# Two layers of a hybrid decoder: the other model of the builder puts the instructions in order

## The chip, the cores and the metric

The kernel runs on one core of a Trainium2 chip. TensorE (PE in the profile) does the matmuls and transposes, VectorE (DVE), ScalarE (ACT) and GpSimd (POOL) the element-wise work, and the queue of SyncE (SP) issues the loads. The metric is device time in microseconds (us), the median of several executions. The builder writes one row of instructions for each engine; in the trace an instruction that waits stands before all that follow it in its row.

## The reference

One step of a decoder with two layers over 560 columns: 32 decoded tokens (8 sequences of 4), 16 meta tokens and a prompt of 512. The channel width is 1024. One layer is:

```
x = x + 0.5 * swiglu(rmsnorm(x), ffn1_w_in, ffn1_w_out)      # inner width 2816
h = rmsnorm(x);  columns = h @ w_mix_in                       # one projection for three groups of heads
fox_o = forgetting attention, 4 heads of 64, bias = sums of log forget gates, paged cache of 512 per sequence
ssd_o = state-space scan, 8 heads of 64 in chunks of 128, causal convolution of width 4, gate, grouped rmsnorm
gla_o = gated linear attention, 4 heads (32, 64), gate per channel, rmsnorm per head, gate
x = x + concat(fox_o, ssd_o, gla_o) @ w_mix_out
x = x + 0.5 * swiglu(rmsnorm(x), ffn2_w_in, ffn2_w_out)
```

The outputs are x for prompt and decoded tokens and, per layer, the new keys, values, log forget gates and the states of the convolution, the scan and the linear attention.

## The kernel before

**Tiling.** x lies transposed in on-chip memory, [128, 8, 560] in fp32: eight blocks of 128 channels. Its columns are two groups, A (304: decode, meta and the first 256 of the prompt) and B (256: the rest). A matrix product is made of three matmuls per block (`mm3`): each operand is split into a high part, rounded to the matmul's input type, and a low part, the rest; high by high, high by low and low by high are summed. `hhiA`, `hloA`, `hhiB`, `hloB` are the parts of the normed activations, `whi` and `wlo` those of a block of weights, `keep` those of blocks that both groups use at a stage's edge. `unit` makes them: a load from SP, a copy on ACT (high), a subtraction on DVE or POOL (low).

**Stages.** Per layer: ffn 1, the mix, ffn 2; then the next layer. An ffn is almost all matmuls. `norm` (and `first_norm` at the start) squares and sums x, multiplies by a column of ones to sum over channels (`ps<-c_ones,s`, one column wide), forms the root on POOL (`nr`), spreads it by a transpose (`ps<-c_ident,nr`), and writes the split activations.

**The mix.** Its steps are generators, run in the order of a hand-written list, a step to each name:

```
MIX_ORDER = """
fox_in:A fox_in:A ssd_in:A fox_in:A gla_in:A gla_in:A O:A gla_in:A fox_norm:A fox_norm:B gla:4 decode:A fox:0
fox:4 gla:0 gla:1 fox:1 ssd_in:A ssd_in:A ssd_in:A ssd:4 ssd:0 ssd:1 gla_in:B gla_in:B gla_in:B ssd_in:B
ssd_in:B ssd_in:B ssd_in:B split:A O:B gla:2 fox:3 ssd:2 gla:3 out:A out:A fox:2 ssd:3 out:A split:B out:A
out:B out:B norm:A out:B out:B norm:B
"""
```

`fox_in`, `ssd_in` and `gla_in` are the input projections (A, B: the group), `fox:`, `ssd:` and `gla:` with a number are the mixers of one tile of columns (0 to 3 the prompt in blocks of 128, 4 decode and meta), `split` splits the mixers' outputs, and `out` is the output projection. The scan (`ssd`) and the linear attention (`gla`) of a tile need the state of the tile before. A mixer's step is a chain: a few matmuls or transposes, DVE or ACT on the result, matmuls again.

**What sets the order.** The program is written for one thread. The builder (`tile.TileContext`) takes the instructions in the order of the program as their order of preference, runs a model of the engines, and puts on each engine's row the first of its instructions that the model says is ready. So the row of an engine is fixed when the program is built, and a wrong guess in the model is not mended on the chip. `BUFS` and the pools of PSUM (two banks of psg for projections, three each of psL and psF for mixers) limit how far ahead it may go.

Nearly all instructions are recorded under the lines of small helpers: L265 matmul (`mm`), L269 transpose (`tr`), L272 and L275 DVE or POOL (`tt`, `stt`), L278 ACT (`act`), L310 POOL's root (`rpow`).

Of the kernel before, what the change touches and what calls it, by code (L numbers as in the profile page):

```python
# [1414 lines left out]
def build():  # L1415
    nc = _bacc.Bacc("TRN2", target_bir_lowering=False, num_devices=1, dynamic_dma_scratch_size=1024)
    a = {n: nc.dram_tensor(n, s, F32, kind="ExternalInput").ap() for n, s in INS.items()}
    a["pt"] = nc.dram_tensor("pt", (1, 32), I32, kind="ExternalInput").ap()
    for n, s in OUTS.items():
        a[n] = nc.dram_tensor(n, s, F32, kind="ExternalOutput").ap()  # L1420
    with tile.TileContext(nc) as tc, ExitStack() as es:
        Trunk(tc, a, es).run()
    nc.finalize()
    return nc
# [61 lines left out]
```

## Time and profile before

| | us |
|---|---|
| median of 3 runs | 2452.31 (2452.1 to 2452.59) |
| profiled execution | 2455.32 |
| its span in the profile | 2453.5 |

The profiled execution is one of its own, 3.0 us above the median of the runs. The page's first section gives busy time per engine; a stretch is read by comparing its length with PE's busy time in it, and by the granted clock beside it, which is 1.00 at 2.4 GHz and 0.5 at 1.2 GHz. By time: ffn 1 of layer 0 until about 450 us, the mix of layer 0 with its projections until 840 us, ffn 2 and the next ffn 1 until 1650 us, the mix of layer 1 until 2060 us, the last ffn until the end.

### The profile page before, as it was taken

The numbers are of one execution on the slowest core, as the hardware profiler recorded it, in microseconds if no ns is written. First come the engines' busy times: TensorE is split into PE (matmuls) and PEld (weight loads), VectorE is DVE, ScalarE is ACT, GpSimd is POOL, SyncE is SP. The second block draws the span as 40 slices with busy tenths as digits, with TensorE's granted clock in tenths as the row PEclk, the third lists the DMA queues.
The fourth block names the chain that finished last, engine by engine and source line by source line (L and its number), as shares of the span: only waits on it lengthen the run. The fifth ranks groups of instructions, "written<-read, shape, count | busy, mean of one in ns | idle before, by whom it ended". The sixth has DMA issues, their size and how long they took to land. (4 is left out here: it accounts for less than half of the span.)

```text
span 2453.5 us, 44862 instructions
## 1 busy us (share of the span) xinstructions
PE 2368.8 (97%) x17908; PEld 2254.9 (92%) x17908; DVE 1256.3 (51%) x2675; ACT 869.7 (35%) x1902; POOL 523.7 (21%) x688
## 2 busy tenths in 40 slices
PE   8999999999889999999999999999998999999999
PEld 8999999987777899999999999999776779999999
DVE  5434345388788533333443333343888985333333
ACT  4323223444354432322333232334343544323231
POOL 3202124233232310100221010131423324101010
PEclk9999999989899999999999999999899999999999
DMA  4222223344322322222222222232443222222222
GB/s 150 88 87 87 87 86 96 95 123 135 116 79 66 106 85 86 87 87 86 87 78 86 86 85 83 87 101 86 129 135 102 88 90 87 87 86 87 87 84 84
DMA packets 89683, 230.57 MB, mean 94 GB/s; under 512 B 12706, under 2 KB 38050, under 8 KB 89474
## 3 DMA queue, kind: packets, MB, share of 16 engines
q1 hardware_dynamic: 89042, 227.54, 29.9%
q8 instruction: 141, 2.31, 0.4%
q14 instruction: 68, 0.56, 0.1%
q10 hardware_dynamic: 432, 0.16, 0.0%
HBM read 219.73 MB, written 7.92 MB: 93 GB/s over the span
## 5 line engine op out<-in xcount | busy, mean ns | idle before, releaser
L272 DVE TENSOR_TENSOR wlo<-raw,whi 128x512 fp32r<-128x512 f32 (+1 forms) x649 | 464.1, 718 | 404.5 <-ACT whi L278 395.1
L278 ACT ACTIVATE whi<-raw 128x512 fp32r<-128x512 f32 (+1 forms) x680 | 427.0, 631 | 646.0 <-PE ps L265 589.3
L265 PE MATMUL ps<-hhiA,wlo 128*128 128x304 f32 x1664 | 507.5, 305 | 0.0
L265 PE MATMUL ps<-hhiA,whi 128*128 128x304 f32 x1664 | 506.8, 305 | 0.0
L265 PE MATMUL ps<-hloA,whi 128*128 128x304 f32 x1664 | 505.6, 304 | 0.0
L265 PE MATMUL ps<-hhiB,wlo 128*128 128x256 f32 x1664 | 471.2, 283 | 4.4 <-POOL wlo L272 3.0
L265 PE MATMUL ps<-hhiB,whi 128*128 128x256 f32 x1664 | 469.6, 283 | 2.0 <-ACT s L278 0.9
L265 PE MATMUL ps<-hloB,whi 128*128 128x256 f32 x1664 | 469.5, 282 | 0.0
L265 PEld LDWEIGHTS ps<-hhiB,whi 128*128 128x128 f32 x1664 | 315.0, 189 | 6.1 <-issue 1.9
L265 PEld LDWEIGHTS ps<-hhiB,wlo 128*128 128x128 f32 x1664 | 315.2, 190 | 5.6 <-POOL wlo L272 3.2
L265 PEld LDWEIGHTS ps<-hhiA,wlo 128*128 128x128 f32 x1664 | 314.8, 189 | 3.9 <-issue 3.0
L265 PEld LDWEIGHTS ps<-hloA,whi 128*128 128x128 f32 x1664 | 315.3, 189 | 2.8 <-issue 2.0
L265 PEld LDWEIGHTS ps<-hhiA,whi 128*128 128x128 f32 x1664 | 314.7, 189 | 2.6 <-issue 1.4
L265 PEld LDWEIGHTS ps<-hloB,whi 128*128 128x128 f32 x1664 | 314.5, 189 | 2.3 <-issue 1.5
L272 POOL TENSOR_TENSOR hidA<-s,hidA 128x304 fp32r<-128x304 f32 x88 | 76.0, 864 | 849.2 <-ACT hidA L278 849.1
L265 PE MATMUL ps<-hidA,whi 128*128 128x304 f32 x1072 | 226.2, 302 | 0.0
L275 DVE SCALAR_TENSOR_TENSOR x<-ps,x 128x304 f32<-128x304 f32 (+1 forms) x192 | 86.0, 449 | 232.3 <-PE ps L265 230.7
L265 PE MATMUL ps<-hidB,whi 128*128 128x256 f32 x1072 | 193.9, 281 | 0.0
L265 PEld LDWEIGHTS ps<-hidA,whi 128*128 128x128 f32 x1072 | 174.4, 188 | 0.0
L265 PEld LDWEIGHTS ps<-hidB,whi 128*128 128x128 f32 x1072 | 166.2, 189 | 0.0
L272 DVE TENSOR_TENSOR s<-s,ps 128x256 f32<-128x256 f32 (+3 forms) x194 | 90.4, 467 | 145.7 <-PE ps L265 137.6
L265 PE MATMUL ps<-hidA,wlo 128*128 128x304 f32 x536 | 162.1, 302 | 0.0
(334 smaller groups left out, 3579.9 us busy)
## 6 DMA issues: line engine op xcount, KB each, us to landing
raw<-win SPq DMA_DIRECT2D x176, 512.0 KB, 3.5
raw<-wout SPq DMA_DIRECT2D x64, 512.0 KB, 3.5
raw<-wfm SPq DMA_DIRECT2D x48, 512.0 KB, 3.5
raw<-wmo SPq DMA_DIRECT2D x32, 512.0 KB, 3.6
raw<-wout SPq DMA_DIRECT2D x32, 384.0 KB, 3.5
pg<-kpage SPq DMA_DIRECT2D x64, 130.0 KB, 2.2
pg<-vpage SPq DMA_DIRECT2D x64, 128.0 KB, 2.3
raw<-wtm SPq DMA_DIRECT2D x8, 544.0 KB
```

The costliest lines, as they stand in the source:

```text
L265: return self.T.matmul(out, lhsT, rhs, start=start, stop=stop, **k)
L272: return (eng or self.V).tensor_tensor(out=out, in0=a, in1=b, op=op)
L275: return self.V.scalar_tensor_tensor(out=out, in0=a, scalar=s, in1=b, op0=op0, op1=op1)
L278: return self.S.activation(out, in_, f, **k)
```

## The change

The builder's other model of the machine is used to make the rows. The instructions, their operands and their data are the same.

```diff
@@ -1418,7 +1418,7 @@
-    with tile.TileContext(nc) as tc, ExitStack() as es:
+    with tile.TileContext(nc, schedule_with_timeline_sim=True) as tc, ExitStack() as es:
         Trunk(tc, a, es).run()
```

On PE, the rows of the ffn stages keep their order but for the ends of a stage. Three places follow, on PE; in a row stands the line, the operation, output<-inputs with the program's numbers, and the size.

The first is at the start, where group B's matmuls with the kept weights run. `ps_354<-c_ones` are the sums of B's norm, `ps_362<-c_ident,nr` its transposes; `ps_366`, `ps_391`, `ps_427` and `ps_452` are projections of the first ffn. Before:

```order
L265 MATMUL ps_366<-hhiB_314,whi_274 128x256
L265 MATMUL ps_366<-hloB_315,whi_274 128x256
L265 MATMUL ps_354<-c_ones_82,s_57_332 128x1
L265 MATMUL ps_354<-c_ones_82,s_58_334 128x1
L265 MATMUL ps_354<-c_ones_82,s_57_332 128x1
L265 MATMUL ps_354<-c_ones_82,s_58_334 128x1
L265 MATMUL ps_366<-hhiB_314,wlo_275 128x256
L265 MATMUL ps_366<-hhiB_314,whi_274 128x256
L265 MATMUL ps_366<-hloB_315,whi_274 128x256
L265 MATMUL ps_366<-hhiB_314,wlo_275 128x256
L269 MATMUL ps_362<-c_ident_80,nr_359 128x128 x2
L265 MATMUL ps_391<-hhiB_314,keep_235 128x256
```

Now:

```order
L265 MATMUL ps_427<-hhiB_314,keep_110 128x256
L265 MATMUL ps_427<-hloB_315,keep_110 128x256
L265 MATMUL ps_354<-c_ones_82,s_57_332 128x1
L265 MATMUL ps_354<-c_ones_82,s_58_334 128x1
L265 MATMUL ps_354<-c_ones_82,s_57_332 128x1
L265 MATMUL ps_354<-c_ones_82,s_58_334 128x1
L265 MATMUL ps_427<-hhiB_314,keep_111 128x256
L265 MATMUL ps_427<-hhiB_314,keep_110 128x256
...
L265 MATMUL ps_452<-hloB_315,keep_97 128x256
L265 MATMUL ps_452<-hhiB_314,keep_98 128x256
L269 MATMUL ps_362<-c_ident_80,nr_359 128x128 x2
L265 MATMUL ps_452<-hhiB_314,keep_97 128x256
```

B's sums now stand some 40 matmuls later, behind `ps_391` and most of `ps_427`, and its transposes come 28 matmuls behind the sums instead of 4.

The second is in the middle of layer 0's mix. `ps_7694`, `ps_7700` and `ps_7704` belong to ssd:0 (`c_strict_r` is a constant mask, `s_1309` and its like come from DVE or POOL), `ps_8039` and `ps_8077` to projections of group B, `ps_8709` to `ps_8722` to fox:3. Before:

```order
L269 MATMUL ps_7694<-c_ident_80,xc_1186_7155 128x128
L265 MATMUL ps_8039<-hloB_4888,whi_8035 128x256
L265 MATMUL ps_8039<-hhiB_4887,wlo_8036 128x256
L265 MATMUL ps_8077<-hhiB_4887,wlo_8070 128x256
L265 MATMUL ps_8077<-hhiB_4887,whi_8069 128x256
L265 MATMUL ps_8077<-hloB_4888,whi_8069 128x256
L265 MATMUL ps_7700<-scz_7698,xc_1186_7155 128x256
...
L265 MATMUL ps_8077<-hloB_4888,whi_8073 128x256
L265 MATMUL ps_8077<-hhiB_4887,wlo_8074 128x256
L265 MATMUL ps_7704<-s_1309_7705,c_strict_r_490 128x512
L265 MATMUL ps_7704<-s_1310_7708,c_strict_r_490 128x512
L265 MATMUL ps_8077<-hhiB_4887,whi_8073 128x256
```

Now:

```order
L269 MATMUL ps_7694<-c_ident_80,xc_1186_7155 128x128
L265 MATMUL ps_7700<-scz_7698,xc_1186_7155 128x256
L265 MATMUL ps_7704<-s_1309_7705,c_strict_r_490 128x512
L269 MATMUL ps_8709<-c_ident_80,f_1538_8701 128x128 x3
L269 MATMUL ps_8716<-c_ident_80,f_1538_8701 128x128
L265 MATMUL ps_8720<-kaug_984,qaug_985 128x400
L265 MATMUL ps_7704<-s_1310_7708,c_strict_r_490 128x512
L269 MATMUL ps_8709<-c_ident_80,f_1539_8703 128x128
L265 MATMUL ps_8722<-kaug_984,qaug_985 128x128
...
L265 MATMUL ps_8722<-c_cmask_r_494,c_identb_978 128x128
L265 MATMUL ps_7714<-s_1313_7715,c_strict_r_490 128x512
L265 MATMUL ps_7714<-s_1314_7718,c_strict_r_490 128x512
```

The projections between the steps of ssd:0 are gone from here (they stand earlier), and steps of fox:3 stand in their place.

The third is the end of layer 0's mix. `ps_9294`, `ps_9304`, `ps_9314`, `ps_9324`, `ps_9332` and `ps_9348` belong to ssd:3, `ps_9454` is an output projection of group A, `ps_9526` and `ps_9562` are two of group B. Before:

```order
L265 MATMUL ps_9294<-s_1708_9295,c_strict_r_490 128x512
L265 MATMUL ps_9294<-s_1709_9298,c_strict_r_490 128x512
L265 MATMUL ps_9454<-hloA_8568,whi_9446 128x304
L265 MATMUL ps_9454<-hhiA_8567,wlo_9447 128x304
L265 MATMUL ps_9454<-hhiA_8567,whi_9446 128x304
L265 MATMUL ps_9454<-hloA_8568,whi_9446 128x304
...
L265 MATMUL ps_9454<-hhiA_8567,wlo_9451 128x304
L265 MATMUL ps_9454<-hhiA_8567,whi_9450 128x304
L265 MATMUL ps_9304<-s_1712_9305,c_strict_r_490 128x512
L265 MATMUL ps_9304<-s_1713_9308,c_strict_r_490 128x512
L265 MATMUL ps_9314<-s_1700_9280,s_1710_9301 128x64 x4
L265 MATMUL ps_9324<-Ssd_71,scz_9288 128x256
```

Now:

```order
L265 MATMUL ps_9290<-scz_9288,xc_1432_8251 128x256
L265 MATMUL ps_9294<-s_1708_9295,c_strict_r_490 128x512
L265 MATMUL ps_9294<-s_1709_9298,c_strict_r_490 128x512
L265 MATMUL ps_9304<-s_1712_9305,c_strict_r_490 128x512
L265 MATMUL ps_9304<-s_1713_9308,c_strict_r_490 128x512
L265 MATMUL ps_9314<-s_1700_9280,s_1710_9301 128x64 x4
L265 MATMUL ps_9324<-Ssd_71,scz_9288 128x256 x2
L265 MATMUL ps_9314<-s_1700_9280,s_1714_9311 128x64 x4
L265 MATMUL ps_9332<-s_1718_9330,sbt_9286 64x256 x2
L269 MATMUL ps_9348<-c_ident_80,s_1701_9282 128x128 x4
L265 MATMUL ps_9526<-hhiB_9426,whi_9518 128x256
L265 MATMUL ps_9562<-hhiB_9426,whi_9554 128x256
```

The output projections of A have moved ahead of this, ssd:3 stands in one piece, and those of B follow it.

## Rows read from the trace of the kernel before

**Rows 1.** The page's span and totals: busy time, share of the span, instructions.

```profile
span 2453.5 us, 44862 instructions
...
PE 2368.8 (97%) x17908; PEld 2254.9 (92%) x17908; DVE 1256.3 (51%) x2675; ACT 869.7 (35%) x1902; POOL 523.7 (21%) x688
```

**Rows 2.** Stretches: length, PE, PEld, DVE, ACT, POOL busy (count), clock, DMA share, GB/s.

```profile
...
420.00:450.00 30.00, 28.70 (x241) 27.97 (x239) 14.54 (x43) 12.81 (x35) 17.87 (x33) 1.00 0.26 72
516.50:608.00 91.50, 86.75 (x668) 66.43 (x667) 75.15 (x216) 34.67 (x95) 34.83 (x78) 0.91 0.45 133
608.00:668.00 60.00, 54.22 (x369) 43.97 (x367) 46.24 (x107) 23.25 (x62) 16.08 (x15) 0.94 0.37 115
668.00:746.60 78.60, 69.98 (x474) 59.80 (x475) 68.62 (x164) 41.08 (x110) 27.75 (x33) 0.93 0.24 78
746.60:791.20 44.60, 40.24 (x254) 31.55 (x252) 36.40 (x77) 20.11 (x56) 12.90 (x13) 1.00 0.21 68
791.20:818.30 27.10, 25.06 (x202) 23.97 (x200) 20.53 (x38) 15.09 (x33) 11.47 (x12) 1.00 0.38 125
818.30:840.00 21.70, 18.22 (x121) 17.48 (x121) 14.81 (x28) 10.47 (x24) 11.07 (x13) 0.92 0.42 136
840.00:1200.00 360.00, 360.00 (x2799) 360.00 (x2798) 133.90 (x236) 106.98 (x204) 36.48 (x43) 1.00 0.29 90
...
1734.00:1827.00 93.00, 85.89 (x672) 65.81 (x671) 75.41 (x224) 36.03 (x99) 33.91 (x78) 0.93 0.45 132
1827.00:1887.00 60.00, 53.78 (x374) 42.41 (x373) 47.78 (x107) 24.42 (x68) 17.15 (x14) 1.00 0.36 116
1887.00:1963.60 76.60, 67.39 (x466) 57.26 (x466) 69.26 (x161) 39.35 (x105) 28.86 (x33) 0.98 0.25 77
1963.60:2008.00 44.40, 40.62 (x255) 31.75 (x253) 37.27 (x77) 20.09 (x55) 12.75 (x13) 1.00 0.20 66
2008.00:2035.00 27.00, 25.30 (x203) 24.06 (x201) 20.54 (x37) 14.79 (x32) 11.65 (x12) 1.00 0.40 131
2035.00:2060.00 25.00, 21.15 (x144) 20.69 (x145) 16.04 (x30) 11.17 (x24) 10.91 (x12) 0.93 0.36 113
```

**Rows 3.** Waits of PE, its timeline and one stretch at the start.

```profile
PE ps L265 <- ACT keep L278: 6.4, 1, 6.4
...
32.41 1.05 PE L265 MATMUL ps<-c_ones,s 128*128 128x1 f32 x8 [1.62 <-DVE s L272]
...
34.90 0.69 PE L269 MATMUL ps<-c_ident,nr 128*128 128x128 f32 x2 [0.85 <-POOL nr L310]
...
35.00:42.00 7.00, 7.00 (x38) 7.00 (x39) 1.78 (x5) 0.90 (x3) 0.00 (x0) 0.58 0.44 150
```

**Rows 4.** Waits of PE in the whole span and at 1200 to 1250 us; that stretch.

```profile
PE ps L265 <- DMA pg<-vpage: 0.4, 1, 0.4
...
PE ps L265 <- DVE s L272: 2.1, 1, 2.1
...
1200.00:1250.00 50.00, 46.86 (x355) 45.95 (x355) 26.50 (x52) 19.37 (x44) 23.20 (x27) 1.00 0.16 53
```

**Rows 5.** The stretch of the middle steps; DVE's timeline at its first and last instruction.

```profile
607.60:717.50 109.90, 96.59 (x641) 80.54 (x641) 90.01 (x213) 51.28 (x135) 34.39 (x40) 0.92 0.32 99
...
656.94 0.41 DVE L275 SCALAR_TENSOR_TENSOR gg<-gg,ps 128x256 f32<-128x256 f32 x1
...
670.53 1.15 DVE L272 TENSOR_TENSOR s<-c_tri,dr 128x512 fp32r<-128x512 f32 x1
```

**Rows 6.** PE's groups in 746.6 to 791.2 us; DVE's timeline there (start, us).

```profile
L265 PE MATMUL ps<-hloA,whi 128*128 128x304 f32 x36 | 11.8, 327 | 0.0
...
744.67 1.02 DVE L1136 TENSOR_SCALAR s<-s,sss 128x256 f32<-128x256 f32 x2
...
790.29 0.62 DVE L1136 TENSOR_SCALAR s<-s,sss 128x256 f32<-128x256 f32 x2 [0.82 <-POOL sss L310]
```

## The prediction

> **What bounds the kernel now.** I read the totals of the page first, then busy time by stretch, then TensorE's (PE's) waits, then single rows. PE is busy 2368.8 us of a span of 2453.5 us [rows 1], so all that an order can change is the idle 84.7 us and the clock at which the rest runs. By stretch, the feed-forward stages are full: 360.00 of 360 us at full clock between 840 and 1200 us, with VectorE (DVE) at 133.90 us [rows 2]. There no order can win, and only a bad one can lose. The idle time lies in both layers' mixing stages. Layer 0's six stretches from 516.5 to 840 us lose 4.75 + 5.78 + 8.62 + 4.36 + 2.04 + 3.48 = 29.03 us (length less PE's busy time), layer 1's six from 1734 to 2060 us 7.11 + 6.22 + 9.21 + 3.78 + 1.70 + 3.85 = 31.87 us [rows 2]. In the same stretches DVE is busy about 80% of the time, and the matmuls that keep PE going are mostly not the mixers' own: they are input and output projections, placed between the mixers' dependent steps. I call them cover. Which of them stand where is what the change decides.
>
> **The change part by part.** Instructions and data are the same; only places in each engine's row differ. The feed-forward stages stand as before, but for their first and last rows. That leaves four kinds of places.
>
> *Start.* PE stops for 1.6 us at group B's first norm (waiting for DVE's s) and for 0.85 us at nr, and then has a stretch of 7 us at a granted clock of 0.58 [rows 3]. The new order puts group B's sum matmuls and transposes some 40 and 65 matmuls later, by which time their inputs are there. If the two stops at B go, and the 7 us behind them come to the full clock (7 × 0.42 = 2.9 us), the start gains up to 1.6 + 0.85 + 2.9 = 5.4 us. Against it, ScalarE and DVE split some kept weights later, behind B's norm; PE already waits once for such a split, 6.4 us [rows 3]; and SyncE's queue issues the second block of input weights behind small constants. Another wait half as long would cost 3.2 us and leave the start at +3 with nothing gained. (Elsewhere loads have slack: all of PE's waits for a DMA in the span are one of 0.4 us [rows 4].) I take −2, between the ends and nearer to the stops that visibly go.
>
> *Norms at the hand-overs.* At 1200 to 1250 us PE loses 3.14 us, of which 2.1 us are one wait for the norm's s [rows 4]; at 420 to 450 us it loses 1.30 us [rows 2]. The norm's matmuls now stand some 20 to 40 rows later. Together at most 4.4 us can go, and nothing shows a loss; I take −3.
>
> *Middle of the mix.* The new order uses projections earlier. After 24 projections in one block, layer 0's row of PE holds ssd:4, fox:1, most of fox:3, ssd:0 and the start of ssd:1 nearly bare: 188 matmuls, 28 of them projections. The same steps were laid out from 607.6 to 717.5 us with 389 projections between them, 0.12 us each, 46.8 us of cover. I counted what the 188 matmuls need. Summed one by one with their full-clock spacing in the trace they are 32.0 us. What DVE has to do in the same piece of its own new row is 119 instructions, the first at 656.94 and the last at 670.53 us of the old trace [rows 5]; their durations there add up to 47.6 us. The mean of the old stretch checks this: 90.01 us for 213 instructions is 0.42 us each, times 119 is 50 us [rows 5]. Layer 1 has the same piece, 158 matmuls (27.7 us) against 109 DVE instructions (41.4 us). So DVE sets the pace there. At no idle time of its own it leaves PE idle 47.6 − 32.0 = 15.6 us and 13.7 us, which is the floor. In the old stretch DVE was busy 90.01 of 109.9 us, a share of 0.82 [rows 5], and at that share the pieces last 58.0 and 50.5 us and leave 26.0 and 22.8 us idle: the other end. I take a share of 0.95, nearer to the floor, since a dependent step no longer queues behind projections on PE: 50.1 − 32.0 = 18.1 us and 43.6 − 27.7 = 15.9 us.
>
> *End of the mix.* gla:3 and ssd:3 now stand one behind the other with 12 projections of out:B near their start, and the other 180 of out:B stand behind ssd:3. Before, 109 projections of out:A lay between the steps (three groups, 36 or 37 each, one shown [rows 6]). In the new row this is 71 matmuls, 17.0 us summed one by one, against 60 DVE instructions, the first at 744.67 and the last at 790.29 us of the old trace [rows 6]. They sum to 29.0 us; the old stretch's mean, 36.40 us over 77 instructions, times 60 gives 28.4 us [rows 2]. At shares of 1, 0.95 and 0.82 (the old stretch has 36.40 of 44.6) the idle time is 12.0, 13.5 and 18.4 us, in each layer.
>
> What is gained in exchange: the norm of A is done inside this gap, and all of out:B stands as cover after it. The idle 2.04 + 3.48 us after 791.2 us, and 1.70 + 3.85 us in layer 1, fall to about 2 us. The first stretch of each mix keeps its 4.75 and 7.11 us: it has more projections than before, but DVE needs 67.8 us there against PE's 61.2 us (summed as above, layer 0), so it can't close. The rest of the middle, between the two bare pieces, is balanced (71.5 us of DVE to 74.0 of PE); I leave 5 us for its chains. One layer then loses 18.1 + 13.5 + 4.75 + 5 + 2 = 43.4 us instead of 29.0 (+14.3), the other 15.9 + 13.5 + 7.1 + 5 + 2 = 43.5 us instead of 31.9 (+11.6).
>
> The sum: 14.3 + 11.6 − 2 − 3 = +20.9 us. The profiled execution took 2455.3 us (1.8 more than its span), so 2476.2 by it; it stands 3.0 us above the median of the runs, 2452.3. I take those 3.0 us off: **2473 us**. With the share at 1 the same sum is 2466, at 0.82 it is 2498.
>
> A place where a rule of the skill bears on this: after stops of 1.6 and 0.85 us the granted clock was 0.58 for 7 us, PE being busy all of them, most of it at 1.2 instead of 2.4 GHz [rows 3]. The Trainium skill, "TensorE: Matmul & The Clock Gate", section "HAM oscillation — how this bites in real kernels", says that a kernel that keeps waiting between short bursts of matmuls is throttled anew at each wait and restarts slowly. By that rule the bare stretches are the worst thing to make, and the second rival below is what would come of it. The trace agrees as to the fall; that PE can also stop without it is seen in the tail, 4.36 us idle at a clock of 1.00 [rows 2].
>
> **The rivals.**
>
> *Faster: the norms gain and the mix cancels.* The mechanism is at the start and at the hand-overs, where PE is the only bound: −5.4 us and −4.4 us, and −3.5 us twice after the mix, −17 us in all. It decides as soon as the bare pieces cost less than that. Up to 791.2 us and 2008 us the mixes now lose 23.5 and 26.3 us; the floors alone, 4.75 + 15.6 + 12.0 and 7.1 + 13.7 + 12.0, are 8.8 and 6.5 us more. If the lower clock of the mixes (0.91, 0.94 and 0.93 over the three stretches up to 746.6 us of layer 0, which is 0.09 × 91.5 + 0.06 × 60 + 0.07 × 78.6 = 17 us) gives 10 of these 15 us back, 2455.3 − 17 + 5 − 3.0 = 2440 us. For it: clock and norm stops are measured. Against it: DVE's floor.
>
> *Much slower: the bare pieces run at the lower clock.* PE's 32.0, 27.7 and twice 17.0 us double to 64.0, 55.4 and 34.0 us. That is longer than DVE's 47.6, 41.4 and 29.0, so PE loses 32.0 + 17.0 and 27.7 + 17.0 us over its full-clock work. With 11.75 and 14.1 us elsewhere the layers rise by 31.7 and 26.9 us: 2455.3 + 58.6 − 5 − 3.0 = 2506 us. For it: 0.58 after the stops at the start. Against it: 1.00 in the tail, with many stops of under 1 us.
>
> *No change.* The feed-forward rows are the same and take over 70% of the span; if the moved cover saves early in the mix what it costs late, 2452 us. For it: the number of projections is the same. Against it: the early part is bounded by DVE too, so cover is worth less there.
>
> **How the numbers follow.** The forecast 0.49, faster 0.21, much slower 0.16, no change 0.14. A change of 0.2% (4.9 us) is about what a measurement of this kernel can tell from none. Slower is the forecast and the second rival, 0.65. The forecast's own range is 2460 to 2498; down to 2440 it takes in no change and half of the faster case, and I stop at 2500, leaving out most of the much slower one.
>
> **What would show it.** In the profile after: the feed-forward stretches full as before; few waits for nr and s at the norms; in each mix a stretch of about 50 us with PE busy under 70% and DVE over 90%, of ssd:4, fox:1, fox:3 and ssd:0, and one of about 30 us with gla:3 and ssd:3; then out:B without a stop. DVE busy under 85% in these stretches says that latency, not DVE's work, is the bound, and the time is above the forecast. A granted clock near 0.5 there speaks for the second rival. PE idle under 60 us in the mixes together, with DVE no denser, would make the prediction wrong: then cover was no bound.

## The result, and the profile after

The changed kernel takes 2529.8 us (median of 4 runs, 2527.57 to 2537.77) against 2452.45 us (4 runs): a ratio of 1.0314, 95% interval [1.0285, 1.0343]. That is 77 us slower where 21 were forecast, outside the range of 2440 to 2500.

The page of the profile after, its span and totals, answers to [rows 1]:

```profile
span 2527.9 us, 44891 instructions
PE 2412.9 (95%) x17908; PEld 2294.0 (91%) x17908; DVE 1274.5 (50%) x2675; ACT 869.6 (34%) x1902; POOL 516.8 (20%) x688
```

The span has grown by 74.4 us. PE's idle time (span less busy) went from 84.7 to 115.0 us, 30 more, and its busy time rose by 44.1 us with the same matmuls, so at a lower clock.

Where this arose is read from six marks that stand in both programs: the first projection of each mix, DVE's last z of each layer's state-space projections, and the first matmul of the ffn after the mix. From the timelines of PE and DVE (start and duration in us), before:

```profile
431.34 0.28 PE L265 MATMUL ps<-whi,hhiA 128*48 128x260 f32 x1
714.27 0.42 DVE L275 SCALAR_TENSOR_TENSOR z<-z,ps 128x256 f32<-128x256 f32 x1
834.63 0.30 PE L265 MATMUL ps<-hhiA,whi 128*128 128x304 f32 x1
1649.48 0.28 PE L265 MATMUL ps<-whi,hhiA 128*48 128x260 f32 x1
1932.13 0.41 DVE L275 SCALAR_TENSOR_TENSOR z<-z,ps 128x256 f32<-128x256 f32 x1
2051.71 0.30 PE L265 MATMUL ps<-hhiA,whi 128*128 128x304 f32 x1
```

and after:

```profile
428.14 0.28 PE L265 MATMUL ps<-whi,hhiA 128*48 128x260 f32 x1
740.08 0.41 DVE L275 SCALAR_TENSOR_TENSOR z<-z,ps 128x256 f32<-128x256 f32 x1
866.59 0.30 PE L265 MATMUL ps<-hhiA,whi 128*128 128x304 f32 x1
1678.21 0.28 PE L265 MATMUL ps<-whi,hhiA 128*48 128x260 f32 x1
1998.57 0.41 DVE L275 SCALAR_TENSOR_TENSOR z<-z,ps 128x256 f32<-128x256 f32 x1
2126.04 0.30 PE L265 MATMUL ps<-hhiA,whi 128*128 128x304 f32 x1
```

The differences between neighbouring marks, beside what the forecast's own terms give for the same stretch:

| stretch | before | after | change | forecast |
|---|---|---|---|---|
| start to the first mix | 431.3 | 428.1 | −3.2 | −2 and a part of the norms' −3 |
| layer 0, first projection to the last z | 282.9 | 311.9 | +29.0 | 18.1 + 4.75 + 5 − 19.15 = +8.7 |
| layer 0, last z to the ffn | 120.4 | 126.5 | +6.2 | 13.5 + 2 − 9.88 = +5.6 |
| ffns and their hand-over | 814.9 | 811.6 | −3.2 | the rest of the −3 |
| layer 1, first projection to the last z | 282.7 | 320.4 | +37.7 | 15.9 + 7.1 + 5 − 22.54 = +5.5 |
| layer 1, last z to the ffn | 119.6 | 127.5 | +7.9 | 13.5 + 2 − 9.33 = +6.2 |
| last ffn | 401.8 | 401.9 | 0.1 | 0 |

Five of the seven rows agree with the forecast to 2 us. But the rows behind a last z do not compare equal work: in layer 0, 751 matmuls and 203 DVE instructions stand between these marks before, and 651 and 169 after; some 100 and 34 of them now stand ahead of the mark. Only a mix as a whole is the same work in both programs, and there the change is +35.2 and +45.6 us against +14.3 and +11.6: the forecast was 55 us short, most of it in the middle. What the end costs for equal work is read from an experiment below.

The bare pieces are longer and look otherwise than was said. By stretch, after (length, then busy time of PE, PEld, DVE, ACT, POOL with counts, granted clock, DMA share, GB/s): the two stretches of each kind in which PE works at no projection, first the middle pieces, then the tails, then an ffn.

```profile
624.60:695.00 70.40, 56.83 (x249) 34.17 (x248) 46.40 (x118) 18.09 (x61) 9.31 (x10) 0.66 0.14 48
1878.60:1949.00 70.40, 57.24 (x228) 36.70 (x227) 43.76 (x111) 17.67 (x60) 8.39 (x8) 0.64 0.14 47
786.10:826.00 39.90, 21.39 (x72) 14.28 (x71) 23.43 (x47) 8.97 (x27) 13.74 (x15) 0.64 0.03 9
2042.70:2085.50 42.80, 24.68 (x80) 16.08 (x77) 26.63 (x50) 9.60 (x29) 15.32 (x17) 0.63 0.02 7
900.00:1200.00 300.00, 300.00 (x2323) 300.00 (x2322) 108.93 (x194) 85.03 (x162) 27.97 (x32) 1.00 0.26 85
```

DVE's 46.40 us in the first piece agree with the 47.6 us that were summed for it. But it takes 70.4 us, DVE is busy 66% of it, PE 81%, and the granted clock is 0.66. The forecast had 50.1 us with 28 projections in it, so about 46.7 for this stretch (0.12 us off for each), at a DVE share of 0.95. The waits in it (us in total, times, longest), two of PE and then two of DVE:

```profile
PE ps L265 <- DVE s L272: 4.5, 4, 1.9
PE ps L265 <- DMA s<-const: 3.2, 1, 3.2
...
DVE smx L821 <- PE ps L265: 8.4, 5, 2.9
DVE s L272 <- PE ps L265: 3.5, 6, 0.7
```

They wait for each other: neither is the bound alone. The one wait for a DMA, a constant whose load is issued at 625.46 us behind four loads of weights in SyncE's row, was not foreseen; [rows 4] had 0.4 us in the whole span. Behind it the clock is at the lower level:

```profile
632.00:642.00 10.00, 10.00 (x32) 5.60 (x33) 3.93 (x10) 1.44 (x5) 0.00 (x0) 0.50 0.17 58
642.00:652.00 10.00, 10.00 (x31) 5.54 (x31) 4.12 (x11) 0.96 (x3) 0.00 (x0) 0.50 0.24 83
```

The start and the hand-over of the ffns answer to [rows 3] and [rows 4]: the 7 us in which B's norm now stands are at the full clock, and the norm's stop at the hand-over is gone.

```profile
35.00:42.00 7.00, 7.00 (x61) 7.00 (x60) 3.98 (x6) 1.95 (x5) 3.67 (x4) 1.00 0.48 173
1230.00:1280.00 50.00, 49.89 (x383) 49.65 (x382) 26.55 (x53) 18.94 (x45) 23.87 (x27) 1.00 0.17 57
```

### The profile page after: what moved, and what is told of

Read it like the earlier page. It is cut to its first block, busy times and chain, and to the rows that moved or that the text cites. A ratio compares the mean times of both kernels' runs of the same rounds, so it can differ in the third digit from the quotient of the medians.

```text
span 2527.9 us, 44891 instructions
## 1 busy us (share of the span) xinstructions
PE 2412.9 (95%) x17908; PEld 2294.0 (91%) x17908; DVE 1274.5 (50%) x2675; ACT 869.6 (34%) x1902; POOL 516.8 (20%) x688
## 4 chain that ended last, share of the span: by engine, by line
PE 89%; DVE 6%; DMA 1%; issue 1%; ACT 1%; POOL 1%; SPq 0%; ACTq 0%; DVEq 0%; POOLq 0%
PE ps L265 88%; PE ps L269 2%; DVE s L272 1%; DVE s L275 1%; DVE g L272 1%; DMA raw<-win 0%; DVE wlo L272 0%; DVE g L275 0%; POOL hloA L272 0%; DMA pg<-kpage 0%; ACT s L278 0%; DMA s<-const 0%; POOL s L272 0%; DVE smx L821 0%; DVE lfp L275 0%
```

## The experiments

All but two of the kernels are the kernel before or the changed one with every engine's row written out: `set_order` ties each instruction to the one before it in a given row (an edge of issue order, no wait), with rows mixed from the two programs.

```diff
         Trunk(tc, a, es).run()
+        set_order(tc, nc)
...
+def set_order(tc, nc):
+    for e, txt in ORDER.items():
+        seq = [names[e][k] for k in np.cumsum(d)]
+        for p, q in zip(seq, seq[1:]):
+            tc.add_manual_dep(q, p.name, ...NoSync...)
```

Theory *chain*: the bare steps depend on each other, so a piece has its length whatever lies between. Theory *clock*: it is long because PE falls to half the clock. Both leave the forecast's reason (DVE's work as the bound) wrong for the piece as a whole. The expectations give 73.6 and 69.3 us for the pieces and 46.5 for the tail; these were read from 639.3, 1894.8 and 797.3 us on and hold projections. The stretches without any are the 70.4, 70.4, 39.9 and 42.8 us above.

**Old mixes, new order elsewhere.** `ORDER`: rows of after, but of before in the two stretches with a mix.

> The rows of all engines are taken from the changed kernel at the start, at the hand-over between the layers' ffns and at the end, and from the kernel before in both stretches that hold a mix (215 to 1000 us and 1450 to 2300 us of the old trace). If the whole loss sits in the mixes, this gives the gains elsewhere alone: 2.0 us at the start and 3.4 us at the hand-over near 1225 us (the same matmuls took 336.6 instead of 340.0 us), so about 2447 us. If the new order also loses somewhere outside, or its gains need its own mixes, about 2452 us or more.

Measured: 2450.3 us (10 runs) against 2453.5 (13 runs), ratio 0.9984 [0.9975, 0.9994]. Its profile at the start and at the hand-over:

```profile
35.00:42.00 7.00, 6.14 (x53) 6.06 (x52) 3.38 (x8) 1.67 (x4) 4.14 (x4) 1.00 0.51 178
1200.00:1250.00 50.00, 49.90 (x389) 49.65 (x388) 27.51 (x54) 20.03 (x46) 24.74 (x27) 1.00 0.16 53
```

So the whole loss is in the mixes, and the gain elsewhere is real, if small: 3.2 us of the expected 5.4. This version is 0.16% ahead of the kernel before.

**Cover in the bare pieces, heavy.** Idle matmuls, tied to a place behind every row of PE in the piece; they write columns of a PSUM bank that nothing reads.

```diff
+    def cover(self, first):
+        if self.n3 in DUPS and first == (self.n3 in FIRST_COVER):
+            h = self.src[:, 0, :]
+            DUPED.append({self.mm(self.bank[:, 272:512], h[:, :128], h[:, :240]).ins.name for _ in DUPS[self.n3]})
```

> The changed kernel's rows, and in the bare piece of each mix one idle matmul (128x128 by 240 columns, into unused columns of a bank, result never read) behind each of 150 and 133 of PE's rows: about 15 and 13 us of PE work at the full clock that depends on nothing late. Theory clock: the pieces take 73.6 and 69.3 us because PE's steps run at half the clock; with cover the clock stays up, the pieces fall to about 55 and 52 us, and the total to about 2495 us. Theory chain: the pieces are a chain of dependent steps whose length has little to do with the clock; the total stays at 2530 or rises by up to 28 us to 2558. A rival to both: the clock stays at half although PE has more to do; then the added work costs double, 56 us, and the total is 2560 to 2585.

Measured: 2580.7 us, 1.0523 [1.0494, 1.0551]. The idle matmuls were not as small as thought: in the piece of layer 0 their group and the stretch read

```profile
L268 PE MATMUL ps<-hhiB 128*128 128x240 f32 x150 | 56.6, 422 | 0.0
...
624.70:719.60 94.90, 86.39 (x397) 57.65 (x397) 45.99 (x118) 18.59 (x62) 8.73 (x10) 0.84 0.11 36
```

56.6 us of added work, not 15, made the piece 24.5 us longer and raised the clock from 0.66 to 0.84. As PE was then 91% busy, this decides nothing between the theories. (The total lies in the range of the third expectation, but by the added work: the clock did not stay at half.) The same in layer 0's tail, three behind each row (`DUPS = {193: ...}`):

> The changed kernel's rows, and in the tail of layer 0's mix alone (gla:3 and ssd:3, 46.5 us at a clock of 0.57) three idle matmuls behind each of 53 rows of PE, 159 in all, about 16 us at the full clock; six projections of out:B move from the tail's start to its end. Theory clock: the tail falls to about 36 us and the total to 2520. Theory chain: the tail keeps its 46.5 us, since its steps wait for each other, and the total is 2530 to 2540.

Measured: 2536.5 us, 1.0337 [1.0318, 1.0357]. The bare tail, from 786.6 to 832.5 us here, became 45.9 us long at a clock of 0.85, with PE busy 34.6 of them where it was 21.4: again the added work stands between the steps, and nothing follows.

**Two buffers for dt and z.** Why did no projection stand in the piece? The first one behind it waits for DVE's z, on the timeline of PE after:

```profile
694.99 0.50 PE L265 MATMUL ps<-hhiB,whi 128*128 128x256 f32 x1 [0.61 <-DVE z L275]
```

The two groups of ssd_in:B that were issued early hold both banks of psg until dt and z of group A, one buffer each, are free behind ssd:1.

```diff
-        dt = R["dt"] = self.t([128, 3, 8], "dt")
+        dt = R["dt"] = self.t([128, 3, 8], "dt", bufs=2)
-                R["z", ti] = self.t([128, 512], f"z{j}")[:tn]
+                R["z", ti] = self.t([128, 512], f"z{j}", bufs=2 if j < 2 else 1)[:tn]
-BUFS = {"s1": 5, "f2": 3, "g2": 8, "s2": 5, "pg": 10}
+BUFS = {"s1": 5, "f2": 3, "g2": 8, "s2": 5, "pg": 6}
```

> The changed kernel with two buffers each for the tiles dt and z of the state-space projections (z of the first two tiles), and six page buffers instead of ten to make room. Theory banks: the bare piece arises since two groups of ssd_in:B hold both PSUM banks of the projections until dt and z of group A are free, behind ssd:1; with a second buffer the order spreads the projections again, the two pieces of 73.6 and 69.3 us lose 20 us each, and the total is about 2490 us. Rival: the model packs the projections early anyway, for instance because it takes matmuls as cheaper than they are; then the pieces stay bare and the total is 2520 to 2530 us.

Measured: 2503.4 us, 1.0195 [1.0178, 1.0212], 26 us less than the changed kernel and 13 more than expected. Layer 0's longest stretch without a projection is now

```profile
659.40:685.80 26.40, 19.33 (x106) 13.31 (x105) 19.64 (x50) 9.95 (x32) 6.87 (x8) 0.73 0.09 31
```

26.4 instead of 70.4 us (in layer 1 the longest is 36.4). The control has the same edit under the old order:

> The control to the kernel with two buffers for dt and z: the same buffers (and six page buffers) under the old order of the kernel before. If the 26 us that two buffers gave under the new model came from freeing the projections' banks, this changes little, 2445 to 2458 us. If two buffers help any order, 2425 to 2440.

Measured: 2468.2 us, 1.0050 [1.0033, 1.0066], slower than before and outside the expected 2445 to 2458: the buffers, or the fewer page buffers, cost something by themselves; the two were not tried apart, under either order. With them the new order loses 35 us against the old one, without them 77.

**Light cover.** `h = self.c("ident_b")`, 128 columns of bf16, in place of the 240: behind each row of the pieces,

> As the earlier cover in the bare pieces, with 150 and 133 idle matmuls, but of bf16 identity by identity (128x128 by 128 columns), since the earlier ones took 0.42 us each in the trace, not 0.1: by the columns these should be some 0.06 us each, 9 and 8 us of PE work. Theory clock: the granted clock in the pieces rises to near 1, the pieces fall from 73.6 and 69.3 us to about 55 and 52, the total to about 2495 us. Theory chain: whatever the clock, the pieces stay within 5 us of their length, total 2525 to 2545. The rival that the clock stays low although PE has more to do: clock 0.5 to 0.7 in the pieces, total 2535 to 2565.

behind each row of the tails, three each,

> The same light idle matmuls in the tails of both layers, three behind each row, 195 or so per tail, about 11 us of PE work at the full clock, and six projections of out:B behind the tail. Theory clock: the clock of 0.57 rises, the two tails of 46.5 us fall to about 36 us, the total to about 2510 us. Theory chain: the tails keep their length, total 2525 to 2545.

only before PE's long waits, in the pieces,

> The changed kernel's rows, with light idle matmuls (bf16 identity, 128 columns) only where PE stood still in the two bare pieces: 128 of them before the eight waits of layer 0's piece (40 before the one of 3.25 us for a DMA, after which the clock fell), 138 before the four waits of layer 1's, so many that they fill about three quarters of each wait and stand in no step's way. Theory clock: PE was busy 61 of 73.6 us in the piece at about half the clock, for work of 32 us at the full one; if the stops are filled, the clock stays near 1 and the pieces fall by 12 to 20 us each, total about 2500 us. Theory chain: the clock comes back but the pieces keep their length, total 2525 to 2535. If the clock falls all the same, the test says nothing on the two, total 2525 to 2540.

in the tails,

> The same in the two tails alone: 142 light idle matmuls before the four long waits (2.8, 2.8, 2.2 and 4.1 us) of gla:3 and ssd:3 in each layer; six projections of out:B stand behind the tail. Theory clock: the clock of 0.57 comes back and each tail of 46.5 us loses 6 to 10 us, total about 2514 us. Theory chain: the clock comes back but the tail keeps its length, total 2525 to 2535, since PE waits for DVE, ACT and POOL there for longer than it works.

and in the pieces before the waits and behind every third row:

> The changed kernel's rows, in the bare pieces the light idle matmuls before the waits as in the run that filled the holes there, and one more behind every third row of PE (50 and 45). Open is how much of the pieces' 73.6 and 69.3 us the clock makes. If the clock now stays near 1 through the pieces and they fall to about 60 us, the clock makes 10 to 14 us of each and the chain of steps by itself takes about 60 us, 10 more than the forecast's 50; total about 2505 us. If they fall to 50 us, the clock was all that the forecast lacked, total about 2490. If they stay at 66 us or more at a clock near 1, the chain is all of it, total 2515 to 2530.

Measured totals: behind each row of the pieces 2554.1 us, 1.0389 [1.0348, 1.0430]; of the tails 2538.1, 1.0331 [1.0281, 1.0381]; holes of the pieces 2518.8, 1.0258 [1.0223, 1.0293]; holes of the tails 2522.7, 1.0281 [1.0244, 1.0319]; holes and every third row 2525.7, 1.0285 [1.0264, 1.0307]. Theory clock had 2495 and 2500 us for the pieces and 2510 and 2514 for the tails; none comes nearer than some 9 us. The two with filled holes alone lie between the theories. The last one lies where its expectation put a piece that keeps 66 us or more, though layer 0's piece fell to 61: layer 1's did not fall. The pieces say more than the totals. Layer 0's piece in these profiles, in this order: every row; tails every row (piece as in after); holes; holes of the tails (piece as in after); holes and thirds.

```profile
626.80:703.00 76.20, 67.56 (x398) 40.56 (x397) 46.63 (x118) 18.39 (x62) 9.34 (x10) 0.91 0.13 45
```

```profile
625.40:697.30 71.90, 57.29 (x249) 34.89 (x248) 46.31 (x118) 18.29 (x61) 9.03 (x10) 0.64 0.14 47
```

```profile
630.30:693.70 63.40, 54.30 (x377) 36.98 (x376) 46.27 (x118) 18.02 (x62) 9.29 (x10) 0.84 0.16 54
```

```profile
624.90:688.60 63.70, 48.54 (x248) 31.31 (x247) 46.30 (x118) 18.29 (x61) 9.01 (x10) 0.79 0.16 53
```

```profile
627.60:688.60 61.00, 52.78 (x426) 35.64 (x425) 46.44 (x118) 18.18 (x62) 8.55 (x10) 1.00 0.17 56
```

The second and the fourth have the same rows in the piece, and differ in the clock: 71.9 us at 0.64, 63.7 at 0.79. (The executions of one program spread as far: those of the run with light idle matmuls in the tails took 2523.6 to 2548.1 us, at mean clocks of 0.966 to 0.956. So the difference need not be one between the programs.) Where the clock counts is seen when the piece is cut at ssd:0's first `ps<-scz,xc`, at 667.1 us after. In this order: after, holes of the tails, holes and thirds, two parts each.

```profile
624.60:667.10 42.50, 35.67 (x147) 20.27 (x146) 22.19 (x63) 9.52 (x33) 0.89 (x2) 0.60 0.24 79
667.10:695.00 27.90, 21.16 (x103) 13.90 (x102) 24.21 (x57) 8.57 (x29) 8.42 (x8) 0.76 0.00 1
624.90:661.10 36.20, 28.58 (x147) 17.78 (x146) 22.18 (x63) 9.91 (x33) 0.93 (x3) 0.76 0.27 93
661.10:688.60 27.50, 19.96 (x101) 13.53 (x101) 24.11 (x57) 8.38 (x28) 8.08 (x8) 0.81 0.00 1
627.60:660.90 33.30, 30.70 (x246) 19.85 (x245) 22.30 (x62) 9.80 (x34) 1.11 (x3) 1.00 0.30 102
660.90:688.60 27.70, 22.08 (x180) 15.79 (x180) 24.14 (x57) 8.37 (x29) 7.44 (x8) 1.00 0.00 1
```

The second part (ssd:0, the rest of fox:3, the start of ssd:1) takes 27.5 to 27.9 us at clocks of 0.76, 0.81 and 1.00, with DVE busy 24.1 to 24.2 us of it: there the steps on DVE set the length, at a share of 0.87. All the difference is in the first part (mostly ssd:4 and fox:1), 42.5, 36.2 and 33.3 us, of which DVE is busy 22.2 or 22.3 each time and PE 84% in the changed kernel.

At 1.00, with 19.1 us of idle matmuls, 128 of 178 in PE's waits, the whole piece is 61.0 us, and DVE is busy 46.4 of it. So in layer 0 the clock makes some 9 us of 70.4, and the chain takes about 61 us by itself where the forecast had 47. Two things blur this by a few us, in opposite directions: the 61.0 us hold 50 idle matmuls between the steps, and PE's wait for the constant is 1.0 us in them instead of 3.2. In layer 1 the clock stayed low with cover too, and how the piece divides there stays open:

```profile
1877.70:1942.80 65.10, 56.31 (x368) 38.09 (x366) 43.09 (x111) 17.51 (x60) 8.00 (x8) 0.76 0.15 51
```

```profile
1873.80:1948.00 74.20, 67.91 (x411) 43.25 (x409) 43.79 (x111) 17.35 (x60) 7.75 (x8) 0.72 0.13 45
```

(holes; holes and thirds). The tails, with idle matmuls behind every row and then with their holes filled:

```profile
787.90:831.80 43.90, 30.60 (x202) 22.67 (x200) 22.49 (x43) 8.55 (x25) 13.74 (x15) 0.74 0.03 8
2042.40:2092.20 49.80, 36.28 (x231) 27.36 (x228) 26.17 (x50) 9.25 (x27) 15.13 (x17) 0.70 0.02 6
778.40:814.50 36.10, 25.23 (x212) 19.46 (x213) 23.03 (x44) 8.40 (x25) 14.11 (x16) 0.86 0.04 11
2035.60:2074.10 38.50, 27.57 (x222) 20.24 (x222) 26.53 (x52) 9.28 (x28) 15.84 (x18) 0.91 0.03 8
```

The first two are longer than after's 39.9 and 42.8 us. The last two are 3.8 and 4.3 us shorter, at clocks of 0.86 and 0.91: less than the 6 to 10 of theory clock, more than the nothing of theory chain. They are still 6 and 8 us above the forecast's 30.5.

**The tail in the old order, and the tail alone in the new.** `ORDER`: rows of after until just behind the bare piece, then what is left in before's order;

> In each mix the changed kernel's rows until just behind the bare piece (740 and 1988 us of its trace), then what is left in the order of the kernel before, so that projections of out:A stand again between gla:3 and ssd:3. Theory cover: the tail's loss (projections used up early) is undone while the bare piece stays; the total falls by the 12 to 15 us that each tail was said to cost, to about 2503 us. Theory chain: the projections are only spread differently and the chain of gla:3 and ssd:3 takes as long; total 2525 to 2535.

and the opposite:

> The opposite of the run with the old tail: the rows of the kernel before until 738 and 1955 us of its trace, then what is left of each mix in the new order, so that out:A's remaining projections come ahead of gla:3 and ssd:3 and these stand bare. Theory chain: gla:3 and ssd:3 keep their 45 us with or without cover, so each layer pays for the moved projections, 109 of 0.14 us or some 10 to 15 us; total 2470 to 2483 us. The forecast's theory (the tail shrinks to about 30 us when the projections are gone) gives 2450 to 2460.

Measured: 2510.8 us, 1.0227 [1.0205, 1.0248], and 2527.5 us, 1.0308 [1.0289, 1.0329]. The first is between the two expectations: 19 us come back. From the last z to the ffn its profile has nearly the work of the changed kernel, 648 and 651 matmuls in layer 0, 673 and 658 in layer 1. Before, after and the old end, all in layer 0, then after and the old end in layer 1:

```profile
714.27:834.63 120.36, 109.39 (x751) 93.54 (x750) 98.82 (x203) 59.20 (x150) 44.65 (x46) 0.99 0.28 91
740.08:866.59 126.51, 104.13 (x651) 91.47 (x649) 87.21 (x169) 52.10 (x124) 40.82 (x45) 0.85 0.26 91
735.12:847.85 112.73, 95.27 (x648) 83.38 (x647) 89.82 (x168) 51.55 (x124) 44.00 (x45) 0.98 0.29 97
1998.57:2126.04 127.47, 105.46 (x658) 93.06 (x657) 87.57 (x168) 52.61 (x127) 41.55 (x45) 0.84 0.26 89
1979.51:2096.12 116.61, 102.98 (x673) 89.60 (x673) 93.01 (x175) 53.11 (x130) 44.87 (x46) 0.96 0.28 93
```

So for about equal work the new order of the end costs 13.8 and 10.9 us, not the +6.2 and +7.9 of the table above. (This execution took 2500.6 us, 10 less than the median; its piece of layer 0 was 63.6 us at a clock of 0.79, so the total does not give the end's price alone.)

The second missed both: it costs 74 us, about three times what was expected. From the last z to the ffn, with the work of before, it takes 156.2 and 153.5 us instead of 120.4 and 119.6, so nearly all of the 74 us lie there. Its profile has layer 0's bare tail and, ahead of it, a second stretch without projections, where the rows of the two programs were joined:

```profile
731.40:752.90 21.50, 14.21 (x78) 9.75 (x78) 9.34 (x24) 5.02 (x15) 2.48 (x2) 0.72 0.08 25
786.00:826.20 40.20, 22.76 (x71) 15.29 (x71) 23.47 (x46) 8.95 (x27) 13.83 (x16) 0.57 0.03 9
```

The bare tail has the 40.2 us of the changed kernel, not the forecast's 30. At a clock of 0.57 this does not tell theory chain from theory clock. The total isn't a price of the tail, since the join has one of its own.

## Why the prediction was wrong

*What bounds the kernel* stood: the ffns did not change (last ffn 401.8 and 401.9 us), and with old mixes the loss is gone.

*Start and hand-overs* were right: −3.2 and −3.2 us against −2 and −3, by the stops that were named. The price of late kept weights was there too, but small: the wait for ACT's keep is 6.7 us where it was 6.4 [rows 3], and that for DVE's, before and after,

```profile
PE ps L265 <- DVE keep L272: 0.6, 1, 0.6
PE ps L265 <- DVE keep L272: 2.1, 2, 1.9
```

rose by 1.5 us.

*End of the mix* looks right, +6.2 and +7.9 us against +5.6 and +6.2, but by luck: some 100 matmuls had left the stretch. For about equal work the end costs 13.8 and 10.9 us. The tail does not shrink to 30 us; without projections it is still 39.9 and 42.8 us long, with DVE busy 59% and 62% of it where the forecast took 95%. This is the failed step of the middle, told next.

*Middle of the mix* has the step that failed. The forecast summed DVE's work rightly (47.6 us; 46.4 in the trace) and then took a DVE share of 0.95, "since a dependent step no longer queues behind projections on PE". The runs refute that reason. With the projections gone the share is 0.66, and with the clock brought back to 1.00 it is 46.4 of 61.0 us, 0.76: lower than the 0.82 of the old stretch [rows 5], which also held the DVE work of the projections; what made it denser there was not tried. Two sums of work side by side, 32.0 and 47.6 us, bound a piece from below; a row of steps in which PE and DVE wait for each other lies nearer to their sum, 79.6 us. Nor do the two sums lie side by side in time: in the second part of the piece DVE reaches 0.87, near the forecast's share, and in the first only 22.3 of 33.3 us even at the full clock, 0.67. Taken over the piece of layer 0, the miss of 23.7 us (70.4 less 46.7) is about 14 us of chain and 9 of clock, the clock's all in the first part. In layer 1 it is some 27 us (70.4 against 43.6), undivided; there 70.4 us at a clock of 0.64 is even above the sum of both engines' work, 69.1.

*The second rival*, bare pieces at the lower clock, described the profile after better than the forecast did: clocks of 0.66, 0.64, 0.64 and 0.63 in the four, and 44.1 us of the 74.4 as busy time of PE. Its 2506 us fell short since it let PE's doubled work take DVE's time with it, where part of them follow each other. By the rule of the Trainium skill, "TensorE: Matmul & The Clock Gate", section "HAM oscillation — how this bites in real kernels", it was the case to expect, and the trace agrees as to the fall: 0.50 behind the wait of 3.2 us. But bringing the clock back gave 4 to 9 us in a piece or a tail, and left layer 0's piece 14 us above the forecast.

*The first rival* fell: the norms gave 6 us, the mixes lost 81.

What the prediction named as signs were the right ones: "DVE busy under 85% in these stretches says that latency, not DVE's work, is the bound, and the time is above the forecast". The range should have reached the sum of both engines' work in the four stretches, 2559 us by the forecast's own terms.

Why the pieces arise at all is shown in part: a second buffer for dt and z shortens layer 0's from 70.4 to 26.4 us and takes 26 us off the total (with four page buffers fewer, which was not tried alone). Why the other model issues ssd_in:B's groups so early was not tried.

## What to carry to other kernels

Independent matmuls between dependent steps are worth what they hide; moved ahead, they leave a chain that does not shrink to the work of the busier engine. Price a stretch that loses its cover between the larger of the engines' work and their sum, take these part by part and not over the whole, and count PE's at the lower clock as well. How long the same steps took with cover is no sure guide: the tail had 44.6 us and kept 39.9, the middle had 109.9 us with 389 projections [rows 5] and kept 70.4. Compare two orders only between marks with equal work. A projection that is issued before its result can be taken out of PSUM holds the bank against all that follow: compare, in the new order, where each group's reader stands.

## What was not expected of the hardware

PE was busy 10.00 of 10 us at a granted clock of 0.50, twice in a row (632 to 652 us after); before, the 7 busy us at 0.58 [rows 3] were followed by 8 at 1.00. In layer 1's piece the clock was 0.64 even with an idle matmul behind every row and PE busy 84 of 95 us; in layer 0's the same cover brought 0.91. The same rows of layer 0's piece ran at 0.64 in one execution and 0.79 in another, 8 us apart.

What an idle matmul cost at a granted clock of 1.00 depended on its neighbours. Behind a single 240-column fp32 one the next row started after 0.20 us (656.05 to 656.25 us, between transposes, in the heavy cover of the pieces) or after 0.31 us (651.26 to 651.57 us); behind three in a row after 0.42 us (820.45 to 820.87 us, in that of the tail), 0.14 each. Projections with 256 columns start 0.12 us apart. Behind a single bf16 one of 128 columns it started after 0.06 us (651.77 to 651.83 us, before a transpose, light ones behind each row of the pieces) or after 0.16 us (650.98 to 651.14 us); 41 in a row took 2.45 us, 0.06 each (631.68 us, holes and thirds). Their busy times in the record, 56.6 us for 150 of the fp32 and 32.8 us for 150 of the bf16 ones, are longer, as a row's recorded end overlaps the start of the next.
